# A layer norm whose loads and stores share one DMA ring in a fixed order, with six tile places of 8 rows

## Chip, cores, metric

One core of one Trainium2 chip. The metric is device time in microseconds (us); most executions of these kernels agree within 0.3%. Profiled spans are some 2 us shorter than timed runs, and spans are compared with spans, times with times. Runs over 1.5% above the fastest of their kernel count as slow and are left out of the ratios.

## The reference

```python
batch, seq, dim = 32, 512, 1024          # x: float32, 67.1 MB
mean = np.mean(x, axis=-1, keepdims=True)
var = np.var(x, axis=-1, keepdims=True)
return ((x - mean) / np.sqrt(var + eps)).astype(np.float32)
```

The result is as large as the input, so 134.2 MB go through the DMA engines.

## The kernel before

The 16384 rows are cut into tiles of K rows for each of the 128 partitions. A tile is loaded into a ring of 48 rows in SBUF, its statistics are taken by VectorE, a few small sums follow on GpSimd, ScalarE normalises it in place, and it is stored from the same place.

```python
TILES = (2, 2, 4) + (8,) * 14 + (4, 2, 2)
RING = 48
# ... place(): gives each tile its rows of x and its place in the ring ...

def rows_of(a, row, K):     # 4*K KiB in a row for each partition
    return a[row * P : (row + K) * P].rearrange("(p k) d -> p k d", p=P)

# ... group(): 2 bn_stats per row (VectorE); GpSimd: mean and sum of squares;
#     ScalarE sqrt; VectorE reciprocal; GpSimd -mean*rstd ...
        for k in range(G):
            nc.scalar.activation(out=xs[:, k, :], in_=xs[:, k, :], func=AF.Identity,
                                 bias=nmr[:, k : k + 1], scale=rstd[:, k : k + 1])

for K, row, pos in place(TILES, RING):
    nc.sync.dma_start(out=ring[:, pos : pos + K, :], in_=rows_of(x2, row, K))   # SP's ring
    for g in range(0, K, GROUP):
        G = min(GROUP, K - g)
        group(ring[:, pos + g : pos + g + G, :], G)
    nc.scalar.dma_start(out=rows_of(o2, row, K), in_=ring[:, pos : pos + K, :]) # ACT's ring
```

Loads are issued by SP and stores by ACT: two queues (DMA rings) that share 16 DMA engines.

## Time and profile before

| | before |
|---|---|
| time, median of 3 runs | 318.33 us (318.19 to 318.66) |
| profiled span | 316.1 us |
| bytes moved | 134.27 MB, 425 GB/s over the span |
| both queues, share of 16 engines | 98.9% |
| first packet begins / last one ends | 1.76 / 314.91 us |

The page gives busy time by engine, then the span in 40 slices (tenths busy), then DMA queues with packets, megabytes and share of the 16 engines. The prediction below shows the lines and how they are read. The *stretch* of a packet is what its duration exceeds the median of its size (309, 611, 1213 ns for 8, 16, 32 KiB); the sum over all packets, divided by 16, is stretch per engine. The *spread* is how far apart the 16 engines finish the same transfer: each ends its share with a 4-byte completion mark, and the marks of a queue, sorted in time, are taken in groups of 16. The records don't name the engine; to follow one engine I lined packets up by end and next start, which may swap two engines that end within a few ns of each other. The spread doesn't depend on that.

### The profile page before, as it was taken

To read this page: it belongs to the slowest core of one execution; us is meant where nothing else is said; L and a number is where in the kernel's file an instruction comes from. 1 tells how busy PE (TensorE), PEld (TensorE's weight loads), DVE (VectorE), ACT (ScalarE), POOL (GpSimd) and SP (SyncE) were. 2 spreads that over 40 slices of the span, in tenths; PEclk is the share of its full clock that TensorE was granted. 3 is DMA by queue.
4 is the path that set the end of the run, shared out by engine and by line. 5 is a ranking of instruction groups with operands and counts; after the bars stand their busy time and mean duration, and the time that the engine had idled before them with its cause. 6 is when DMAs were issued, how large, how long until landed. Compare 5 with 4: busy or idle time off the path is not lost.

```text
span 316.1 us, 794 instructions
## 1 busy us (share of the span) xinstructions
DVE 157.1 (50%) x277; ACT 154.3 (49%) x149; POOL 45.1 (14%) x204
## 2 busy tenths in 40 slices
DVE  2368596547092561916529074190652908363030
ACT  1336296692833809247091561900651956196321
POOL 0420202201102020020200202002020020221120
DMA  7999999999999999999999999999999999999996
GB/s 301 433 399 469 431 416 425 433 427 444 420 448 419 444 419 444 435 427 444 419 448 415 448 424 440 423 448 419 444 423 440 423 435 429 446 428 417 455 411 282
DMA packets 5766, 134.27 MB, mean 425 GB/s; under 512 B 640, under 2 KB 640, under 8 KB 640
## 3 DMA queue, kind: packets, MB, share of 16 engines
q1 hardware_dynamic: 2880, 67.11, 49.6%
q10 hardware_dynamic: 2880, 67.11, 49.3%
q14 instruction: 6, 0.05, 0.0%
HBM read 67.11 MB, written 67.11 MB: 425 GB/s over the span
## 4 chain that ended last, share of the span: by engine, by line
DMA 58%; DVE 17%; ACT 9%; POOL 6%; issue 3%; another core or an unknown queue 3%; ACTq 0%; POOLq 0%; DVEq 0%; SPq 0%
DMA ring<-in_x_dram 32%; DMA out_dram<-ring 27%; DVE stats L75 17%; ACT ring L111 8%; POOL half L64 1%; ACT std L103 1%; POOL dev L97 1%; POOL nmean L87 1%; POOL dev L100 1%; POOL dev L90 1%; POOL dev L96 1%; POOL nmean L67 1%; POOL ss L67 1%; DVE rstd L107 0%
## 5 line engine op out<-in xcount | busy, mean ns | idle before, releaser
L75 DVE BATCH_NORM_STATS2 stats<-ring 128x6 f32<-128x512 f32 x256 | 153.7, 678 | 71.2 <-DMA ring<-in_x_dram 71.2
L111 ACT ACTIVATE ring<-ring,nmr,rstd 128x1024 f32<-128x1024 f32 x128 | 147.0, 1227 | 10.8 <-POOL nmr L109 10.8
L103 ACT ACTIVATE std<-ss,eps_t 128x8 f32<-128x8 f32 (+2 forms) x20 | 6.0, 300 | 143.0 <-POOL ss L67 115.8
L107 DVE RECIPROCAL rstd<-std 128x8 f32<-128x8 f32 (+2 forms) x20 | 3.9, 193 | 77.3 <-ACT std L103 77.3
L64 POOL TENSOR_TENSOR half<-stats 128x16 f32<-128x16 f32 (+2 forms) x20 | 4.5, 226 | 221.0 <-DVE stats L75 221.0
L109 POOL TENSOR_TENSOR nmr<-nmean,rstd 128x8 f32<-128x8 f32 (+2 forms) x20 | 4.0, 202 | 27.2 <-DVE rstd L107 27.2
L97 POOL TENSOR_SCALAR dev<-dev 128x32 f32<-128x32 f32 (+2 forms) x20 | 5.6, 281 | 1.8
L100 POOL TENSOR_TENSOR dev<-dev,stats 128x32 f32<-128x32 f32 (+2 forms) x20 | 4.9, 243 | 1.7
L90 POOL TENSOR_TENSOR dev<-stats,nmean 128x32 f32<-128x32 f32 (+2 forms) x20 | 4.6, 231 | 1.7
L87 POOL TENSOR_SCALAR nmean<-nmean 128x8 f32<-128x8 f32 (+2 forms) x20 | 4.6, 228 | 1.8
L96 POOL TENSOR_TENSOR dev<-dev 128x32 f32<-128x32 f32 (+2 forms) x20 | 4.6, 228 | 1.6
L64 POOL TENSOR_TENSOR half<-dev 128x16 f32<-128x16 f32 (+2 forms) x20 | 4.2, 210 | 1.6
L67 POOL TENSOR_TENSOR nmean<-half 128x8 f32<-128x8 f32 (+2 forms) x20 | 4.0, 199 | 1.6
L67 POOL TENSOR_TENSOR ss<-half 128x8 f32<-128x8 f32 (+2 forms) x20 | 4.0, 199 | 1.6
L103 ACT ACT_TABLE_LOAD x1 | 1.3, 1283 | 0.9 <-DVE eps_t L120 0.9
L120 DVE MEMSET eps_t<- 128x1 f32 x1 | 0.1, 59 | 0.8 <-PEq L143 0.8
L143 POOL MEMSET const-float32-0.0<- 128x1 f32 x1 | 0.1, 98 | 0.2 <-issue 0.2
L143 POOL MEMSET const-uint8-127<- 128x1 uint8 x1 | 0.1, 102 | 0.0
L143 POOL MEMSET const-bfloat16-1.0<- 128x1 bf16 x1 | 0.1, 101 | 0.0
L143 POOL MEMSET const-float32-1.0<- 128x1 f32 x1 | 0.1, 98 | 0.0
## 6 DMA issues: line engine op xcount, KB each, us to landing
ring<-in_x_dram SPq DMA_DIRECT2D x14, 4096.0 KB, 47.3
out_dram<-ring ACTq DMA_DIRECT2D x14, 4096.0 KB, 40.7
ring<-in_x_dram SPq DMA_DIRECT2D x4, 1024.0 KB, 30.8
ring<-in_x_dram SPq DMA_DIRECT2D x2, 2048.0 KB, 27.2
out_dram<-ring ACTq DMA_DIRECT2D x4, 1024.0 KB, 16.7
out_dram<-ring ACTq DMA_DIRECT2D x2, 2048.0 KB, 24.5
```

The lines of the kernel that those rows point to most:

```text
L64: nc.gpsimd.tensor_tensor(out=half[:, :G], in0=terms[:, :, 0:2], in1=terms[:, :, 2:4], op=ALU.add)
L67: nc.gpsimd.tensor_tensor(out=o, in0=half[:, :G, 0], in1=half[:, :G, 1], op=ALU.add)
L75: nc.vector.bn_stats(out=stats[:, k, s, :], in_=xs[:, k, s * BN_MAX : (s + 1) * BN_MAX],)
L87: nc.gpsimd.tensor_scalar(out=nmean[:, :G], in0=nmean[:, :G], scalar1=-1.0 / H, scalar2=None, op0=ALU.mult)
L90: nc.gpsimd.tensor_tensor(out=dev[:, :G], in0=mean4, in1=nmean[:, :G].unsqueeze(2).to_broadcast([P, G, H]), op=ALU.add,)
L96: nc.gpsimd.tensor_mul(out=dev[:, :G], in0=dev[:, :G], in1=dev[:, :G])
L97: nc.gpsimd.tensor_scalar(out=dev[:, :G], in0=dev[:, :G], scalar1=float(D // H), scalar2=None, op0=ALU.mult)
L100: nc.gpsimd.tensor_tensor(out=dev[:, :G], in0=dev[:, :G], in1=m2, op=ALU.add)
L103: nc.scalar.activation(out=std[:, :G], in_=ss[:, :G], func=AF.Sqrt, bias=eps_t, scale=1.0 / D)
L107: nc.vector.reciprocal(out=rstd[:, :G], in_=std[:, :G])
L109: nc.gpsimd.tensor_mul(out=nmr[:, :G], in0=nmean[:, :G], in1=rstd[:, :G])
L111: nc.scalar.activation(out=xs[:, k, :], in_=xs[:, k, :], func=AF.Identity, bias=nmr[:, k : k + 1], scale=rstd[:, k : k + 1],)
```

## The change

Loads and stores are put into one ring, SP's, in a written order; every tile has 8 rows but the last two; the ring has six whole places; the small tiles of statistics get a pool with enough buffers for all. The intent is an order of transfers that is known in advance and never leaves the queue dry.

```diff
-TILES = (2, 2, 4) + (8,) * 14 + (4, 2, 2)
+TILES = (8, 8, 8, 8, 8, 8, 8, 8, 8, 8, 8, 8, 8, 8, 8, 4, 4)
+ORDER = "LLLLSLSLSLSLSLSLSLSLSLSLSLSLLSSSSS"
...
+    sm = ctx.enter_context(tc.tile_pool(name="sm", bufs=len(TILES) + N // P // GROUP))
...  (half, nmean, dev, ss, std, rstd, nmr: from st, 4 buffers, to sm)
-        for K, row, pos in place(TILES, RING):
-            nc.sync.dma_start(out=ring[:, pos : pos + K, :], in_=rows_of(x2, row, K))
-            for g in range(0, K, GROUP):
-                G = min(GROUP, K - g)
-                group(ring[:, pos + g : pos + g + G, :], G)
-            nc.scalar.dma_start(out=rows_of(o2, row, K), in_=ring[:, pos : pos + K, :])
+        loads, stores = iter(plan), iter(plan)
+        for op in ORDER:
+            if op == "L":
+                K, row, pos = next(loads)
+                nc.sync.dma_start(out=ring[:, pos : pos + K, :], in_=rows_of(x2, row, K))
+            else:
+                K, row, pos = next(stores)
+                for g in range(0, K, GROUP):
+                    G = min(GROUP, K - g)
+                    group(ring[:, pos + g : pos + g + G, :], G)
+                nc.sync.dma_start(out=rows_of(o2, row, K), in_=ring[:, pos : pos + K, :])
```

More of the change, by code (lines that the diff above doesn't have):

```diff
@@ L7 @@
 from concourse._compat import with_exitstack
-TILES = (2, 2, 4) + (8,) * 14 + (4, 2, 2)
+TILES = (8, 8, 8, 8, 8, 8, 8, 8, 8, 8, 8, 8, 8, 8, 8, 4, 4)
 RING = 48
 GROUP = 8
-def place(tiles, ring):
-    plan, row, pos = [], 0, 0
-    for K in tiles:
-        if pos + K > ring:
-            pos = 0
-        plan.append((K, row, pos))
-        row += K
-        pos += K
-    return plan
+ORDER = "LLLLSLSLSLSLSLSLSLSLSLSLSLSLLSSSSS"
 @with_exitstack
@@ L45 @@
     NSUB = D // BN_MAX
+    H = 2 * NSUB
     assert sum(TILES) * P == N
@@ L62, in pool_sum @@
         G = terms.shape[1]
-        half = st.tile([P, GROUP, 2], fdt, name="half")
+        half = sm.tile([P, GROUP, 2], fdt, name="half")
         nc.gpsimd.tensor_tensor(
@@ L78, in group @@
                 )
-        H = 2 * NSUB
         parts = stats[:, :G].rearrange("p g s (h c) -> p g (s h) c", h=2)
         mean4, m2 = parts[:, :, :, 1], parts[:, :, :, 2]
-        nmean = st.tile([P, GROUP], fdt, name="nmean")
-        dev = st.tile([P, GROUP, H], fdt, name="dev")
-        ss = st.tile([P, GROUP], fdt, name="ss")
+        nmean = sm.tile([P, GROUP], fdt, name="nmean")
+        dev = sm.tile([P, GROUP, H], fdt, name="dev")
+        ss = sm.tile([P, GROUP], fdt, name="ss")
         pool_sum(nmean[:, :G], mean4)
@@ L101, in group @@
         pool_sum(ss[:, :G], dev[:, :G])
-        std = st.tile([P, GROUP], fdt, name="std")
+        std = sm.tile([P, GROUP], fdt, name="std")
         nc.scalar.activation(
@@ L105, in group @@
         )
-        rstd = st.tile([P, GROUP], fdt, name="rstd")
+        rstd = sm.tile([P, GROUP], fdt, name="rstd")
         nc.vector.reciprocal(out=rstd[:, :G], in_=std[:, :G])
-        nmr = st.tile([P, GROUP], fdt, name="nmr")
+        nmr = sm.tile([P, GROUP], fdt, name="nmr")
         nc.gpsimd.tensor_mul(out=nmr[:, :G], in0=nmean[:, :G], in1=rstd[:, :G])
@@ L117, in group @@
             )
+    plan, row, pos = [], 0, 0
+    for K in TILES:
+        if pos + K > RING:
+            pos = 0
+        plan.append((K, row, pos))
+        row += K
+        pos += K
     with tc.manual_schedule():
         nc.vector.memset(eps_t, eps_val)
-        for K, row, pos in place(TILES, RING):
-            nc.sync.dma_start(out=ring[:, pos : pos + K, :], in_=rows_of(x2, row, K))
-            for g in range(0, K, GROUP):
-                G = min(GROUP, K - g)
-                group(ring[:, pos + g : pos + g + G, :], G)
-            nc.scalar.dma_start(out=rows_of(o2, row, K), in_=ring[:, pos : pos + K, :])
+        loads, stores = iter(plan), iter(plan)
[9 more added lines that the diff above has]
+                nc.sync.dma_start(out=rows_of(o2, row, K), in_=ring[:, pos : pos + K, :])
 _INS = ['x', 'eps']
```

## The prediction

> **What bounds the kernel now.** I read the page in this order: busy shares, the 40 slices, the DMA queues; then the time windows, the waits of the engines, the waits of the SP queue; last the trace's packet records. The busy shares and slices first, because they say which engine could be the bound:
>
> ```profile
> DVE 157.1 (50%) x277; ACT 154.3 (49%) x149; POOL 45.1 (14%) x204
> ...
> DMA  7999999999999999999999999999999999999996
> GB/s 301 433 399 469 431 416 425 433 427 444 420 448 419 444 419 444 435 427 444 419 448 415 448 424 440 423 448 419 444 423 440 423 435 429 446 428 417 455 411 282
> ...
> q1 hardware_dynamic: 2880, 67.11, 49.6%
> q10 hardware_dynamic: 2880, 67.11, 49.3%
> ```
>
> No compute engine is busy half of the time, while the DMA row has a 9 in every slice but the first and the last. The two queues (q1 loads, q10 stores) took 49.6 + 49.3 = 98.9% of the 16 engines' span: 312.6 of 316.1 us. Only 3.5 us per engine are not packets. The windows (columns: stretch, its length, busy time of DVE, ACT and POOL, clock, DMA share, GB/s) say that this is a flat plateau and not an average over different stages:
>
> ```profile
> 40.00:80.00 40.00, 26.60 (x46) 26.00 (x25) 6.76 (x29) 1.00 1.01 434
> 80.00:120.00 40.00, 19.79 (x35) 19.65 (x20) 4.85 (x21) 1.00 1.00 432
> 120.00:160.00 40.00, 19.58 (x34) 20.22 (x20) 4.64 (x20) 1.00 1.00 433
> 200.00:240.00 40.00, 19.29 (x33) 15.62 (x15) 4.43 (x19) 1.00 1.00 433
> ```
>
> The waits agree. VectorE's only large wait is for loads, and the SP queue, which issues the loads, waits for stores to free ring places:
>
> ```profile
> DVE stats L75 <- DMA ring<-in_x_dram: 71.2, 13, 7.3
> ...
> SPq L122 <- DMA out_dram<-ring: 215.6, 12, 19.0
> ```
>
> 215.6 us of waiting looks like something to remove. It isn't: while SP waits, the DMA engines are busy with what was issued earlier. A wait of an issuer costs only if the engines behind it run dry, and share 1.00 says that they don't.
>
> The packet records carry the rest. A packet is one partition's rows of a tile: 32 KiB for 8 rows, 16 KiB for 4, 8 KiB for 2. Median durations are 1213, 611 and 309 ns, the same for loads and stores, in the loads-only start, in the mixed middle and in the stores-only end. 32768 B / 1213 ns x 16 = 432 GB/s. Lining up packets by their ends, each engine's next packet begins where the last one ended; in the mixed middle an engine alternates between a load packet and a store packet without a gap. The first packet starts at 1.76 us; the last ends at 314.90 us, and the span ends 1.2 us later. The 16 engines finish between 313.2 and 314.9 us.
>
> **What the Trainium skill says.** "DMA: Bandwidth & Descriptors", section "Issuing engines are not separate DMA queues": DMAs issued from SP, ACT or GpSimd run on the same 16 engines, and issuing from several saves only issue time on the sequencer. The trace agrees: two queues together make 432 to 434 GB/s, and one queue alone, at the start, has the same packet time. Same page, "Where 436 GB/s comes from": a fabric ceiling of 435.2 GB/s. The plateau, 432 to 434, is within 1% of it. Same page, "Queues, rings and completion order": each engine takes turns between the rows it has work for, packet by packet; descriptors within one ring are consumed in order and carry no barrier. The first half is what the alternation shows; the second is what the change will lean on. Same page, "Two DMAs through the same engine are not ordered": being on one queue doesn't order a load behind an earlier store, so a semaphore wait must still protect each ring place. The instruction order of the changed kernel has these waits: each load from the seventh on waits for a store's completion.
>
> **The change, part by part.**
>
> (a) Stores move from ACT's queue to SP's. ACT loses 20 issues at a median of 338 ns = 6.8 us. It is busy 49% and never sets the end: gain 0. SP gets 34 issues of about 0.33 us = 11 us over 316: no bound.
>
> (b) One ring instead of two. The bytes are unchanged, 67.1 MB each way. Engine time is counted in packets: before, per engine, 2 x (14x8x1213 + 2x8x611 + 4x8x309) ns = 311.04 us, with 40 completion marks of 9 ns = 0.36. After, 2 x (15x8x1213 + 2x8x611) = 310.67 and 34 marks = 0.31. Difference: -0.42 us. That is all that tile sizes are worth in engine time.
>
> (c) The tile sizes 2, 2, 4 at the start give way to 8. First compute starts later (before, stats began at 5.69 us), which matters only if the queue runs dry before the first store is ready. Four loads come first: with 8 packets x 1.21 us = 9.7 us per slot they occupy the engines from 1.8 to 40.6 us. Tile 0 lands at about 1.8 + 9.7 + 0.9 = 12.4 us. Its way to the store, by the rows of an 8-row tile of before (stats at 24.61, next tile's store at 47.10): statistics 9.6, GpSimd chain with its hops 2.9, square root to first scaling 0.85, eight scalings 9.2: 22.5 us. Store 0 is ready at about 35 us, in the queue by 37. Margin: some 3.5 us. Tile 1's store: VectorE goes in order, so a tile costs it 9.6 + 3.3 = 12.9 us (measured, 37.51 to 50.44), and store 1 is ready near 48; its slot is the sixth after the start (store 0, load 4 lie ahead), at 60. Store 2: 61 against 79. The margin grows by 6.5 us a tile, as a pair of slots takes 19.4 us and a tile's compute 12.9.
>
> (d) The fixed order in the steady state. Load j ends in slot 2j-3; its store has slot 2j+4. Six slots lie between, 58 us, for a latency of some 25: 33 us to spare. Load j reuses the place of store j-6, which ends four slots (39 us) before the load's slot. So SP should always be two or more transfers ahead of the engines, and the ring of six tiles suffices.
>
> (e) The end. Load 16 is followed by stores 12 to 16, i.e. 3 x 9.7 + 2 x 4.85 = 39 us of work. Tile 16 needs some 13 us of compute, all under it. Before, the last tile was scaled as late as 309.1 us, yet its engines had store work until 313 to 315, so little is won here: at most the spread of the engines' ends, 1.7 us.
>
> (f) Small tiles in a pool with 33 buffers: removes reuse waits that the list of waits doesn't show. 0.
>
> Sum: 316.1 - 0.4 (b) - 0 to 1 (spread of ends, stretched packets) = about 315.5 us of span. The timed median lies 2.2 us above the profiled span; so 317.8 us.
>
> **The rivals.**
>
> R1: direction changes in one ring cost time. If an engine had to drain its writes at each of some 28 switches from load to store or back, with the completion mark between, 0.3 us each would add 8 us (326), 1 us each 28 us (346). For it: no stretch of before has both directions in one ring; and the load packets around the entry of the first stores were stretched (about 60 of them between 15.9 and 22.4 us, by 0.1 to 0.3 us). Against: before, each engine switches direction at nearly every packet, some 300 times, with no gap; and inside the loads-only start the boundaries between two transfers with a completion mark show none either.
>
> R2: less switching helps. If the mix cost anything, whole tiles in one direction would beat it. Against: packet times are equal in mixed and unmixed stretches. The most to be won from the ceiling of the page cited is 134.2 MB / 435.2 = 308.4 us of packets against about 311 (my estimate): 2.5 us or 0.8%, within 2% still.
>
> R3: head of the line. A store at the head that isn't ready blocks loads behind it, where two queues would let loads pass. By (c) only store 0 is close; if its latency were 5 us more, some 1.5 us would be lost, once: 319.5. A slot order wrong in the middle would repeat, but the margin there is 33 us.
>
> **Range and chances.** The engines are busy 98.9% before and must move the same bytes after; a gain above 2% (6.4 us) exceeds everything that isn't packets, 3.5 us. Hence 0.01. A loss above 2% needs R1 at 0.25 us or more per switch, or R3 in the steady state: 0.03. Point 317.8 us; low 316.6 (no spread at the end, no stretched packets), high 319.6 (the start's margin used up).
>
> **What would show it.** The DMA row again full 9s with a single queue of about 98 to 99% share and 134 MB; the windows at 432 to 434 GB/s; packets of 32 KiB at 1213 ns; the DVE still waiting for loads; the first store issued near 35 us with the windows from 35 to 45 us at full rate. Wrong would be: packets longer than 1213 ns or gaps at the switches (R1), GB/s above 436 (R2), a dip in DMA share near 40 us or repeated every 19 us (R3).

## The result

322.38 us median (321.76 to 322.90, 4 runs) against 318.26 us for the kernel before (4 runs). The ratio is 1.0128, 95% interval 1.0107 to 1.0149. Here and below a ratio is the mean time of one kernel's fast runs over that of the other's of the same rounds, so not quite the ratio of the medians. The result is within 2%, but 4 us slower and outside the range of 316.6 to 319.6.

The page of the changed kernel, span 319.6 us, the parts that answer to those of before (the 40 slices and the queue):

```profile
DVE 156.4 (49%) x274; ACT 152.9 (48%) x146; POOL 39.2 (12%) x174
...
DMA  8999999999999999999999999999999999999993
GB/s 328 431 422 451 402 395 451 410 439 428 427 435 415 439 426 422 455 406 451 406 447 439 418 436 427 422 451 406 451 418 439 443 414 422 443 435 447 418 418 168
...
q1 hardware_dynamic: 4896, 134.22, 98.2%
```

Nothing ran dry: 9s throughout, and, as I lined packets up, no gap beyond 303 ns between packets of an engine. But packets took 98.2% of 319.6 = 313.8 us per engine, where before it was 312.6, although nominal packet time fell by 0.4. And 5.8 us per engine are not packets, against 3.5 before; the last slice (168 GB/s against 282) says where. The list of what SP waits for (waiter, releaser, us in total, times, longest) shows the new order at work, and no wait that leaves the DMA engines idle:

```profile
SPq L130 <- ACT ring L102: 199.5, 16, 22.5
SPq L124 <- DMA out_dram<-ring: 51.9, 8, 7.1
```

The windows (length, then DVE, ACT, POOL, clock, DMA share, GB/s) of the last microseconds, first of the kernel before:

```profile
313.00:314.00 1.00, 0.00 (x0) 0.00 (x0) 0.00 (x0) 1.00 0.53 221
314.00:315.00 1.00, 0.00 (x0) 0.00 (x0) 0.00 (x0) 1.00 0.10 41
315.00:316.00 1.00, 0.00 (x0) 0.00 (x0) 0.00 (x0) 1.00 0.00 0
```

and of the changed kernel:

```profile
313.00:314.00 1.00, 0.00 (x0) 0.00 (x0) 0.00 (x0) 1.00 0.81 344
314.00:315.00 1.00, 0.00 (x0) 0.00 (x0) 0.00 (x0) 1.00 0.50 213
315.00:316.00 1.00, 0.00 (x0) 0.00 (x0) 0.00 (x0) 1.00 0.31 131
316.00:317.00 1.00, 0.00 (x0) 0.00 (x0) 0.00 (x0) 1.00 0.04 16
317.00:318.00 1.00, 0.00 (x0) 0.00 (x0) 0.00 (x0) 1.00 0.08 33
```

Half of the engines have finished by 314.5, and from 316.4 us a single one is still storing. A share of 0.08 is about one engine of 16. The Trainium skill, "DMA: Bandwidth & Descriptors", section "Why a DMA increments its semaphore by 16 and not by 1", says that the engines of a transfer finish independently and that only the full count means that all has landed; so the slowest engine sets the end. The windows of the middle say that the plateau is a little lower until 220 us, and then the same as before. Changed kernel:

```profile
60.00:140.00 80.00, 40.58 (x72) 42.40 (x42) 11.58 (x50) 1.00 1.00 429
140.00:220.00 80.00, 39.18 (x68) 39.15 (x38) 9.25 (x40) 1.00 1.00 430
220.00:300.00 80.00, 39.36 (x69) 43.03 (x42) 11.21 (x50) 1.00 1.00 433
```

Kernel before:

```profile
60.00:140.00 80.00, 39.40 (x70) 39.22 (x38) 11.60 (x50) 1.00 1.00 433
140.00:220.00 80.00, 38.97 (x67) 36.46 (x35) 9.08 (x39) 1.00 1.00 433
```

The DMA share doesn't see it, as a stretched packet counts as busy; GB/s does.

The packet records, changed kernel, first profile, in us:

```
                                      before    changed
last engine ends                      314.91    318.34    +3.43
mean of the 16 ends                   313.79    315.01    +1.22
last engine behind the mean             1.12      3.33    +2.21
stretch per engine                      1.14      2.96    +1.82
  first 5 us / 5 to 50 / after 50   .22/.60/.32  .60/.94/1.42
```

Of the 127 stretched packets (over 40 ns too long) 124 are loads and 3 are stores. 16 of them are the first packets of the program. Nearly all the others sit near 40, 60, 80, 99, 119, 158, 178, 197 and 216 us: in the last two packets of a load, just ahead of a store in the ring. The other change, from store to load, shows nothing. At each of these changes the spread grows:

```
end of transfer near (us)    42   52   61   81  100  120  159  188  217  245  314
spread of 16 engines (us)  0.62 0.89 1.27 1.83 2.59 3.40 3.74 4.52 4.74 4.74 4.74
```

In the kernel before the loads end between 1.8 and 1.3 us apart from 65 to 182 us, and 2.2 us from 201 us on.

My theory from here on, T1: a single ring in which the direction changes lets the engines delay one another at each change from load to store. Rivals: T2, the tile sizes or the ring of six places; T3, the last loads collide with the compute engines' accesses to SBUF.

### The profile page after: what moved, and what is told of

It is laid out like the page before. It is cut to its first block, busy times and chain, and to the rows that moved or that the text cites. A ratio compares the mean times of both kernels' runs of the same rounds, so it can differ in the third digit from the quotient of the medians.

```text
span 319.6 us, 730 instructions
## 1 busy us (share of the span) xinstructions
DVE 156.4 (49%) x274; ACT 152.9 (48%) x146; POOL 39.2 (12%) x174
## 3 DMA queue, kind: packets, MB, share of 16 engines
q1 hardware_dynamic: 4896, 134.22, 98.2%
## 4 chain that ended last, share of the span: by engine, by line
DMA 60%; DVE 17%; ACT 10%; POOL 4%; issue 2%; ACTq 0%; SPq 0%; POOLq 0%; DVEq 0%
DMA ring<-in_x_dram 45%; DVE stats L67 16%; DMA out_dram<-ring 15%; ACT ring L102 10%; POOL half L56 1%; ACT std L94 0%; POOL dev L88 0%; POOL dev L91 0%; POOL dev L81 0%; POOL nmean L78 0%; POOL dev L87 0%; ACTq L161 0%; POOL nmean L59 0%; POOL ss L59 0%; DVE rstd L98 0%
## 5 line engine op out<-in xcount | busy, mean ns | idle before, releaser
L94 ACT ACTIVATE std<-ss,eps_t 128x8 f32<-128x8 f32 (+1 forms) x17 | 5.1, 299 | 133.2 <-POOL ss L59 133.2
L56 POOL TENSOR_TENSOR half<-stats 128x16 f32<-128x16 f32 (+1 forms) x17 | 3.9, 232 | 230.0 <-DVE stats L67 230.0
L98 DVE RECIPROCAL rstd<-std 128x8 f32<-128x8 f32 (+1 forms) x17 | 3.4, 200 | 54.5 <-ACT std L94 54.5
L88 POOL TENSOR_SCALAR dev<-dev 128x32 f32<-128x32 f32 (+1 forms) x17 | 4.8, 284 | 1.5
L100 POOL TENSOR_TENSOR nmr<-nmean,rstd 128x8 f32<-128x8 f32 (+1 forms) x17 | 3.5, 203 | 11.2 <-DVE rstd L98 11.2
L91 POOL TENSOR_TENSOR dev<-dev,stats 128x32 f32<-128x32 f32 (+1 forms) x17 | 4.3, 254 | 1.4
L81 POOL TENSOR_TENSOR dev<-stats,nmean 128x32 f32<-128x32 f32 (+1 forms) x17 | 4.0, 238 | 1.4
L78 POOL TENSOR_SCALAR nmean<-nmean 128x8 f32<-128x8 f32 (+1 forms) x17 | 4.0, 235 | 1.5
L87 POOL TENSOR_TENSOR dev<-dev 128x32 f32<-128x32 f32 (+1 forms) x17 | 4.0, 235 | 1.3
L56 POOL TENSOR_TENSOR half<-dev 128x16 f32<-128x16 f32 (+1 forms) x17 | 3.6, 212 | 1.3
```

Source lines behind the costliest of these rows:

```text
L56: nc.gpsimd.tensor_tensor(out=half[:, :G], in0=terms[:, :, 0:2], in1=terms[:, :, 2:4], op=ALU.add)
L78: nc.gpsimd.tensor_scalar(out=nmean[:, :G], in0=nmean[:, :G], scalar1=-1.0 / H, scalar2=None, op0=ALU.mult)
L81: nc.gpsimd.tensor_tensor(out=dev[:, :G], in0=mean4, in1=nmean[:, :G].unsqueeze(2).to_broadcast([P, G, H]), op=ALU.add,)
L87: nc.gpsimd.tensor_mul(out=dev[:, :G], in0=dev[:, :G], in1=dev[:, :G])
L88: nc.gpsimd.tensor_scalar(out=dev[:, :G], in0=dev[:, :G], scalar1=float(D // H), scalar2=None, op0=ALU.mult)
L91: nc.gpsimd.tensor_tensor(out=dev[:, :G], in0=dev[:, :G], in1=m2, op=ALU.add)
```

## The experiments

Five rounds each (three for the last two), beside the kernel before on the same chip, whose medians lay between 318.08 and 318.26 us.

### The changed kernel again

No edit.

> The changed kernel unaltered, for a second profile and a time on the same chip as the next runs. In its first profile the last two packets of each load, those just ahead of a store in the same ring, were stretched beyond 1213 ns (2.95 us per engine in all, 1.14 us in the kernel before), and the 16 engines finished 4.7 us apart (1.7 before). If this is a property of the kernel and not of one run: 322 to 323 us, total stretch 2.5 to 4 us per engine, nearly all of it in loads, ends 3.5 to 6 us apart. If it was chance, 318 us and ends some 2 us apart.

Measured: 322.68 us (322.03 to 322.99), ratio 1.0142. Stretch 3.38 us per engine, 132 of 136 stretched packets are loads, ends 4.6 us apart. It came again in full, so it is no chance of one run.

### Two rings, all else as changed

```diff
-                nc.sync.dma_start(out=rows_of(o2, row, K), in_=ring[...])
+                nc.scalar.dma_start(out=rows_of(o2, row, K), in_=ring[...])
```

> The changed kernel with its stores back on ACT's queue: tile sizes, ring of six, pool and order of compute stay. Theory T1 (a single ring stretches the loads at each change from load to store): 317.5 to 318.5 us, stretch about 1 us per engine, ends under 2.5 us apart. Theory T2 (the 8-row tiles at the start and end, or the ring of six, cost it): stays at 322 us.

Measured: 318.70 us (318.42 to 318.98), ratio 1.0015 (1.0003 to 1.0027). Windows of its end:

```profile
312.00:313.00 1.00, 0.00 (x0) 0.00 (x0) 0.00 (x0) 1.00 0.99 426
313.00:314.00 1.00, 0.00 (x0) 0.00 (x0) 0.00 (x0) 1.00 0.16 66
314.00:315.00 1.00, 0.00 (x0) 0.00 (x0) 0.00 (x0) 1.00 0.04 16
```

And of its middle, where the plateau is whole:

```profile
60.00:140.00 80.00, 40.77 (x72) 42.27 (x42) 11.57 (x50) 1.00 1.00 433
140.00:220.00 80.00, 38.98 (x67) 34.81 (x33) 9.05 (x39) 1.00 1.01 434
```

The last engine ends at 314.84 us. From 50 us on the stretch is 0.10 us per engine (1.42 and 1.71 in the single ring), and the ends are 1.7 us apart. The first packets (0.62 us) and the entry of the first store (0.68 us between 30 and 50 us) are stretched here too. So one word in one line brings back all but 0.4 us (0.1 to 0.9 by the interval). T2 falls: the other parts together (tiles, ring of six, pool) cost no more than that. The edit does two things at once: it ends the changes of direction within a ring, and it lets each engine mix load and store packets, where one ring makes all engines go through whole transfers in one direction. Which of the two matters this run doesn't say; the two runs with mixed rings below bear on it.

### Half as many changes of direction

```diff
-ORDER = "LLLLSLSLSLSLSLSLSLSLSLSLSLSLLSSSSS"
+ORDER = "LLLL" + "SSLL" * 6 + "L" + "SSSSS"
```

> One queue, but after the four first loads the order is two stores, two loads, and so on: 7 changes from load to store instead of 13, the same packets. T1 with a cost per change: of the 2.95 us of stretch 0.6 belongs to the first packets and 0.9 to the first change; the other 1.4 us halve, and the spread with them: 320 to 321.3 us. If only being one ring matters and not the count of changes: 322.4. If T2: 322.4.

Measured: 321.08 us (320.99 to 321.33), ratio 1.0090. Stretch after 50 us 0.69, half of 1.42, as a cost per change would have it; but the ends still lie 4.3 us apart. The time is within the expected range, but the spread, which sets the end, didn't halve.

### No compute

```diff
-                    group(ring[:, pos + g : pos + g + G, :], G)
+                    pass
```

Its output is wrong, which doesn't matter for the time.

> The changed kernel without statistics and scaling (its output is x, wrong on purpose): loads and stores on the one queue in the same order, no traffic of VectorE, ScalarE and GpSimd to SBUF. T1 (a matter of the DMA ring alone): stretched packets at the changes remain, 321 to 323 us. Theory T3 (the last load packets collide with the compute engines' accesses to SBUF): the stretch goes, 317.5 to 318.5 us.

Measured: 321.26 us (320.09 to 321.97), ratio 1.0092. Stretch 3.48 us, 144 of 145 stretched packets loads, ends 5.1 us apart. T3 falls: the stretch is there in full without any compute. The time is 1.4 us shorter than with it, though, and the two don't overlap; I have no reason for that.

### Loads and stores in turn in both rings

```diff
+(nc.sync, nc.scalar)[pos // 8 % 2].dma_start(...)      # for loads and for stores
```

> Both rings, but each carries loads and stores in turn: tiles of the even ring places are loaded and stored by SP, those of the odd ones by ACT. Each ring changes from load to store 6 or 7 times. If a change within a ring costs as such: 320 to 321.5 us, ends 4 us apart. If it costs only where the engine has no other ring's packets to put between: 317.8 to 319 us, ends about 2 us apart. Loads issued from ACT may also hold up scaling; that would show as idle DMA engines and not as stretched packets.

Measured: 326.58 us over all six executions, 323.39 to 327.77 in the four fast ones (up to 335.53 in the two slow ones). The start spoilt the time: tiles 0 and 1 were now loaded side by side, tile 0 landed at 22 instead of 13 us, the first store came late, and the engines stood still:

```profile
40.00:45.00 5.00, 5.00 (x9) 5.00 (x5) 0.00 (x0) 1.00 0.14 59
```

After 70 us there was hardly any stretch, and the spread stayed at 1.5 to 2.4 us. That looked as if an engine is safe as long as the other ring has a packet to put between; the run "Both rings mixed, without the gap at the start" below tests it.

### Twice the changes, with packets of half the size

```diff
-TILES = (8, ..., 8, 4, 4)
+TILES = (4,) * 32
-ORDER = "LLLLSL..."
+ORDER = "L" * 8 + "SL" * 24 + "S" * 8            # 25 changes
+ORDER = "L" * 8 + "SSLL" * 12 + "S" * 8          # the pair of it: 13 changes
-    sm = ... bufs=len(TILES) + N // P // GROUP
+    sm = ... bufs=33
```

> One ring, 32 tiles of 4 rows, eight loads first, then store and load in turn: 25 changes from load to store instead of 13, packets of 16 KiB at 611 ns, which alone make 312.8 us per engine against 310.7, so 2.1 us more. If the cost grows with the count of changes (321.1 us at 7, 322.5 at 13: 0.23 us each): 322.5 + 2.1 + 2.8 = 327.4 us. If not: 324.6 us.

> As the run before, but two stores and two loads in turn: 13 changes, as in the changed kernel, with 16 KiB packets: 324.6 us by the count of changes. The difference to the run before is the effect of the count alone, 2.8 us if it is linear, 0 if the count doesn't matter.

Measured: with 25 changes 321.83 us (ratio 1.0115), with 13 changes 322.65 us (1.0139). More changes were faster by 0.8 us, not slower by 2.8. My floor was also too high: the records of neighbouring packets overlap by 3 to 4 ns, so the step is 607 ns and 1209.5 ns, and the smaller packets cost 512 x 607 - 256 x 1209.5 = 1.2 us, not 2.1. With 1.2 us taken off:

```
changes load->store      7      13 (two profiles)    13 (4-row)   25 (4-row)
last engine ends       317.7     318.3, 318.6           318.1        317.6
spread at the end        4.3       4.7, 4.6               4.9          4.0
```

The price doesn't go with the count, though 7 changes took less time than 13 with the same packets (321.08 against 322.68 us). In the run of 25 changes the spread rose to 3.3 us by 130 us and then stood still through 30 transfers. So T1 in its first form, a price per change, was wrong too. New form, theory L (lockstep): engines that arrive at a change together delay one another, which drives them apart; once they are some 4 us apart, changes are nearly free. Its rival, theory C: a constant price per change.

### Halves

Each transfer as two of 64 partitions, store half and load half in turn (the order rewritten for it, not shown).

> One ring, 8-row tiles, but each transfer is issued as two of 64 partitions, and store and load halves alternate: 4 packets of 32 KiB per engine between changes, 25 changes. By the count: 322.5 + 2.8 = 325.3 us; if the cost depends on how long a run of loads came before and shorter runs cost less per change: 322 to 323 us. A transfer of 64 partitions may load the 16 engines otherwise than one of 128; packets other than 1213 ns all through would show that.

Measured: 461.3 us over all six executions, 451.71 and 456.41 in the two fast ones. A failed experiment: packets took 1381 ns at the median and 1731 in the mean, and the windows show half the rate from the first load on:

```profile
0.00:40.00 40.00, 9.85 (x18) 4.44 (x5) 2.53 (x14) 1.00 0.98 205
40.00:80.00 40.00, 19.59 (x34) 18.80 (x19) 4.66 (x20) 1.00 1.00 209
```

It says nothing on the changes, and much on transfers of 64 partitions.

### Engines set apart from the start

```diff
                 nc.sync.dma_start(out=ring[:, pos : pos + K, :], in_=rows_of(x2, row, K))
+                if row == 0:
+                    for at, n in ((0, 12), (12, 8), (20, 4)):
+                        nc.sync.dma_start(out=ring[at : at + n, 40 : 40 + R, :],
+                                          in_=rows_of(x2, 0, R)[at : at + n])
```

with R = 8 (32 KiB a packet) and R = 4. The place is tile 5's and is overwritten by its load.

> The changed kernel with three small extra loads after the first load, of 12, 8 and 4 partitions of 32 KiB each, into a place of the ring that is overwritten later: some of the DMA engines get one, two or three packets more than others, so they are set apart by up to 3.6 us from the start. Theory L (lockstep: engines that come to the change from load to store together delay one another, until they are far enough apart): the stretch after the first packets falls from 2.5 us per engine to under 1.2, and the ends lie hardly further apart than before (4 to 6 us); the time stays near 322 to 323 because the extra packets cost the latest engines 3.6 us themselves. Theory C (each change costs the same whatever the spread): stretch stays at 2.5 us and the ends lie 6 to 8.5 us apart, 325 to 326 us.

> The same with extra packets of 16 KiB: set apart by up to 1.8 us. Theory L: stretch between the run before and the changed kernel, 1.2 to 2.2 us beyond the first packets, ends 4 to 5 us apart, 322 us. Theory C: 2.5 us, ends 6 us apart, 324 us.

Measured: 331.98 us and 326.15 us, far over what I expected, because the small transfers themselves were slow: stretch of 10.3 and 4.6 us per engine between 5 and 30 us. The times therefore decide nothing. What follows after 30 us does:

```
                        spread at    spread    stretch per engine
                        about 32 us  at end    after 30 us
changed kernel             0.6        4.7       2.35  (second profile 2.79)
set apart, R = 4           2.1        5.3       1.38
set apart, R = 8           4.0        5.5       0.25
```

(32 us here means: before the first change.) With R = 8, where the engines are 4 us apart, the same 13 changes in the same ring go with a tenth of the stretch, and in the windows the plateau is whole:

```profile
60.00:140.00 80.00, 44.84 (x79) 47.30 (x45) 11.11 (x48) 1.00 1.00 433
140.00:220.00 80.00, 40.93 (x72) 37.83 (x36) 9.34 (x40) 1.00 1.00 433
```

This run is as theory L has it; C wanted 2.5 us of stretch and ends 6 to 8.5 us apart. Two things in the records speak against L in this form. The changed kernel itself, near 216 us, with its engines 4.5 us apart, still has 0.24 us of stretch per engine at one change, no less than the 0.18 near 60 us, where they are 0.9 us apart. And R = 4 has to be held against the control further down.

### Both rings mixed, without the gap at the start

```diff
+    def ring_of(row): return (nc.sync, nc.scalar)[row // 8 % 2]
-                nc.sync.dma_start(out=ring[...], in_=...)
+                (nc.sync if row < 32 else ring_of(row)).dma_start(out=ring[...], in_=...)
-                nc.sync.dma_start(out=rows_of(...), in_=...)
+                ring_of(row).dma_start(out=rows_of(...), in_=...)
```

> Both rings with loads and stores in turn as in the earlier mixed run, but the first four loads all go through SP, so that tile 0 lands early and the gap of 4.7 us near 45 us goes. If what protects the two-ring kernel is that each engine always has another ring's packet to put between: stretch only up to about 70 us, ends about 2 us apart and the spread not growing, 318.3 to 319.5 us. If a change within a ring costs in any case: 320.5 to 322.

Measured: 324.81 us over all six executions, 323.48 to 324.99 in the four fast ones, ratio 1.0191; a clear miss. Stretch 6.4 us per engine and 1.2 us of gaps, at nearly every change. In this profile both rings change direction at the same time, every 20 us: store 2 lands with load 5 at 92.8 us, load 6 with store 3 at 112. In the earlier mixed run the two rings changed at different times and there was no stretch after 70 us. So "a packet of the other ring in between" isn't what protects; two rings that never change direction do, in every run here. Why simultaneous changes of two rings cost so much, and open gaps, stays open.

### Small tiles first, two rings

```diff
+TILES = (2, 2, 4) + (8,) * 14 + (4, 4)
+                nc.scalar.dma_start(out=rows_of(o2, row, K), in_=ring[...])
```

(Order: six loads, thirteen pairs of store and load, six stores; SP holds loads only.)

> A candidate for the best: two rings, ring of six places as now, tiles 2, 2, 4 first as in the kernel before and 4, 4 at the end. Against the two-ring run it should win back the slow first packets (0.6 us of stretch against 0.22 with 8 KiB packets): 318.0 us, 0 to 0.2 us under the kernel before.

Measured: 318.26 us (317.96 to 318.75), ratio 1.0002 (0.9990 to 1.0013). The 0.4 us of the two-ring run seem to come back, but not by the term I named: the first packets were stretched by 0.57 us here as well, and the stretch in all, 1.33 us, is nearly that of the two-ring run, 1.40. The two intervals also overlap. It doesn't beat the kernel before; nothing here does.

### Control: the extras without the offsets

```diff
+                    for at in (0, 16, 32):
+                        nc.sync.dma_start(out=ring[at : at + 16, 40:48, :], in_=rows_of(x2, 0, 8)[at : at + 16])
```

> Control of the offset runs: the same place in the program, but each of the three extra loads has 16 partitions, so that every engine gets three packets more and none is set apart on purpose. Theory L (engines set apart don't delay one another at the changes): the engines stay within 1 to 2 us of one another up to the first change, and the stretch from 30 us on is 1.5 us per engine or more, as in the changed kernel (1.9 and 1.8 in its two profiles), not 0.2 as with the 3.6 us offsets. If the extra transfers themselves took the stretch away: 0.5 us or less from 30 us on. If these small transfers spread the engines anyway, the spread before the first change says which case it is.

Measured: 335.91 us. Same disturbance of the start (10.3 us of stretch between 5 and 30 us), but a spread of 0.53 us before the first change. After 30 us the stretch was 1.21 us, under the 1.5 that I asked for and well over 0.25; the spread went from 0.5 to 6.3 us, where the set-apart run went from 4.0 to 5.5. The plateau shows it too, if by little:

```profile
60.00:140.00 80.00, 42.06 (x74) 47.30 (x45) 11.13 (x48) 1.00 1.01 431
140.00:220.00 80.00, 40.05 (x71) 37.83 (x36) 9.34 (x40) 1.00 1.00 432
```

The expectation quotes 1.9 and 1.8 us for the changed kernel after 30 us; by the measure used here it is 2.35 and 2.79. What is missing is the first change: 0.07 us of stretch between 30 and 50 us against 0.94, though the engines were in step. I have no reason for that. All three runs with extras lack it, so they are fairly compared after 50 us only:

```
                        spread before     stretch per engine
                        first change      after 50 us
changed kernel             0.6            1.42  (second profile 1.71)
control, even              0.5            1.14
set apart, R = 4           2.1            1.28
set apart, R = 8           4.0            0.19
```

So the extras alone took part of the stretch away. Setting the engines 2 us apart took away nothing more; only the run with 4 us stands out, by a factor of six, in one profile and on another chip than its control.

### Brought into step again in the middle

```diff
+ORDER = "LLLL" + "SL" * 4 + "SSSS" + "LLLL" + "SL" * 5 + "SSSS"
+        if row == 64:
+            pos -= 8          # tile 8 takes the place of tile 7 and waits for its store
```

> One ring, but tile 8 is loaded into the place of tile 7, so that its load waits for the last of the stores before it: the queue runs dry once, near 165 us, and all 16 engines start again together; four loads follow as at the start. Theory L: the second half pays again, stretch after the restart 1.2 us per engine or more, most of it at its first changes, and the spread, back under 1 us after the restart, grows again to 2.5 us or more. Time 322.5 + 4 to 6 for the dry stretch + some 2 = 329 to 331 us. If only the start of the program has the stretch: under 0.5 us of stretch after the restart, 327 us.

Measured: 326.83 us (324.77 to 327.55). Slices of its page:

```profile
DMA  8999999999999999999699999999999999999996
GB/s 325 438 410 451 442 395 414 434 426 427 430 434 423 442 430 422 446 430 422 272 373 406 455 442 402 391 451 422 426 434 434 418 442 408 440 424 436 426 422 260
```

The 6 in the DMA row is the dry stretch, 3.8 us per engine. The dip of the sixth slice (395, at 40 to 48 us, the first change) comes again some 20 slices later as 402 and 391, at the first change after the restart. From the records: spread 2.9 us at 158 us, 0.54 after the restart, 0.83 at 212, 1.66 at 261, 2.45 at the end; stretch after 175 us 1.6 us per engine, 0.7 of it between 200 and 210 us. In the changed kernel the stretch after 175 us is 0.49 us (0.35 in the second profile). So the cost returns after the restart. But the restart brings back more than the step of the engines: four loads in a row, and the first change after them. That first change has 0.9 of the 1.6 us (190 to 210 us), and the two-ring run pays at its first change too (0.68 us). What is left after 210 us is 0.69 us, against 0.26 and 0.28 in the changed kernel. The spread ended just under the 2.5 I asked for, and the time 2 us under my sum.

## Why the prediction was wrong

- **What bounds the kernel**: right. DMA engines busy without a break, before and after.
- **(a), (c), (d)**: right in what they claim. The first store was issued at 35.6 us (about 35 predicted), the second at 48.5 (near 48), and no queue ran dry. ACT's freed 6.8 us bought nothing. The first packets were slower than before, 0.60 us of stretch against 0.22 in the first 5 us, but the larger first tile is not shown to be the reason: with small tiles first it was 0.57.
- **(b)**, -0.4 us of nominal packet time: right by its arithmetic, with the bare durations unchanged at 1213 and 611 ns; it drowned in what follows. Since the records of neighbouring packets overlap by 3 to 4 ns, and each engine has 48 packets fewer now, my estimate today is nearer -0.25.
- **(e) and the sum**, the term "0 to 1 (spread of ends, stretched packets)", counted as a gain: this is the step that failed. I took the spread of the engines as a leftover that could only shrink. It is part of the bill: the last engine lies 3.33 us behind the mean instead of 1.12, and the mean itself is later by 1.2 us, as stretch rose by 1.8. Sign and size were wrong: the last engine ended 3.4 us later, where I had 0 to 1 us earlier. The sum itself is also loose: 316.1 - 0.4 - (0 to 1) is 314.7 to 315.7, and 315.5 lies near its upper end.
- **R1**, behind the 0.03 that I gave to a loss above 2%, was the right rival by place: load packets just ahead of stores. I even named the "about 60" stretched packets near 16 to 22 us in the trace of before (45 by the measure of 40 ns), and set them aside. The argument against it, "before, each engine switches direction at nearly every packet, some 300 times, with no gap", was read from a state that doesn't occur in one ring: two rings, each in one direction. And R1's form, a price for each of some 28 switches, was wrong as well: the order has 25 of them, only the 13 changes from load to store show a cost, and it isn't a fixed price for each (7, 13, 25 changes: last end 317.7, 318.3 to 318.6, 317.6 us).
- **R2** and **R3**: rightly rejected; over stretches of 80 us GB/s stays at 429 to 433, and no dip recurs every 19 us from a blocked head.

What is shown: putting loads and stores into a single ring causes it (322.7 against 318.7 us, one line changed); the stretch needs no compute; it isn't a fixed price per change. What is only inferred: that the delay is between engines, and that engines far enough apart are spared. One run is as that theory has it (4 us apart); the run at 2 us, the late changes of the changed kernel and the first change of the even control are not, and the restart can be read in two ways. So theory L is not shown. What is open: whether a change of direction within a ring is enough (two mixed rings that changed at different times showed no stretch after 70 us), what the engines contend for, why only the last two load packets are hit, why the even control had no stretch at its first change, and why two mixed rings that change together are worst.

## What to carry to other kernels

On a kernel that is bound by DMA, look at more than busy share and GB/s: the end is set by the slowest of 16 engines, so compare packet durations with their median and see how far apart the engines finish. Try loads in one ring and stores in another first, although both share the engines; an order of transfers fixed in one ring cost 1.3% here, and the wait that it replaces cost nothing. Evidence that something is free, taken from a steady state, holds for that state alone: ask whether the change leaves it.

## What the Trainium skill lacked or had wrong

- "DMA: Bandwidth & Descriptors", "Issuing engines are not separate DMA queues" and the row on spreading DMAs over issuers in "Rules for kernel authors": on this page they allow only the sequencer's issue time as a gain. Here issue time was no bound, and loads on SP with stores on ACT took 318.70 us against 322.68 for the same transfers on SP alone.
- Same page, "Queues, rings and completion order": nothing on what a change of direction within a ring costs. Here 124 of 127 stretched packets were loads, after the start nearly all of them the last two ahead of a store, up to 1041 ns over 1213; the reverse change showed nothing.
- Same page: it says that the engines finish independently, not how far apart they drift. Here it was 1.7 to 2.6 us at the end in three kernels with loads in one ring and stores in the other, 4.0 to 5.1 us in single rings without extras or a restart.
- No page: records of neighbouring packets overlap by 3 to 4 ns, so that the step of a 16 KiB packet is 607 ns where its record says 611; over 512 packets that is 2 us.
